# A two-layer encoder trunk on one core: another order of the seven products of a pair, and four powers on GpSimd at the start

## The chip, the core and the metric

The kernel runs on one core of one Trainium2 chip. The metric is the device time of one execution in microseconds. Five engines of the core matter here, each with an instruction queue of its own: TensorE (in profiles PE, with its weight loads as PEld), VectorE (DVE), ScalarE (ACT), GpSimd (POOL) and SyncE (SP), which here only issues DMAs. They wait for each other through semaphores. SBUF is the working memory, PSUM the memory into which TensorE writes, in banks.

## The reference

A trunk of two layers over 512 tokens of width 1024, in float32, with a memory of 256 tokens. Cut to what matters:

```python
for layer in range(2):
    xn = rms_norm(x, mix_norm[layer])
    x = x + (fox_diff_mixer if layer == 0 else mlstm_mixer)(xn, ...)
    x = x + memory_cross_attention(rms_norm(x, ...), rms_norm(mem, ...), ...)
    x = x + conv_ffn(rms_norm(x, ffn_norm[layer]), w_up, conv_w, conv_b, w_down)
return rms_norm(x, final_norm)

def conv_ffn(xn, w_up, conv_w, conv_b, w_down):
    h = causal_depthwise_conv(xn @ w_up, conv_w) + conv_b   # three taps along the tokens
    g, u = jnp.split(h, 2, axis=-1)                         # 2816 columns each
    return (jax.nn.gelu(g) * u) @ w_down
```

The change touches `conv_ffn`, in both layers, and the start of the program. `rms_norm` multiplies by the mean square to the power -0.5.

## The kernel before

**Numbers.** To keep float32 accuracy each operand is split into a high part, rounded to the float32r type, and a low part, the rest. ScalarE makes the high part by a copy (`split`, L282, or the casts at L1183 and L1352), VectorE the low part by a subtraction (`sub`, L279). A product of two operands is three matmuls (`mm3`, L289 to L291): high by high, high by low, low by high. Nearly every subtraction on VectorE has both of its inputs in SBUF.

**Start.** `constants()` makes the identity (on GpSimd), a tile of ones and a few others, and twelve small products on ones for TensorE to start with. Then the first mixer loads x, forms xh and xl (L491 on ScalarE, L492 on VectorE), the weights of the gates (L541 to L546) and the first value product, until the norm's factor is known. The powers of -0.5 of the norms are worked out on VectorE (`rsqrt`, L425 to L432): a first guess from the bits and three Newton steps, on a few columns. GpSimd makes causal masks in the mixers (L900, L1574), a few memsets, and in the feed-forward stage issues the DMAs that add one block of weights onto another (L1336).

**Feed-forward.** The 2 x 2816 columns of `w_up` are 22 pairs of blocks of 128, one block of g and one of u. A pair is computed in one of two ways. `plain` does two ordinary blocks of 8 x 3 matmuls over 512 tokens. `seven`, for the 16 pairs listed in SEVEN, sees the pair as a 2 x 2 block product (block g or u by half of the inner dimension, times half of the inner dimension by half of the tokens) and does it with seven products in place of eight, after Strassen and Winograd. A product is 4 x 3 matmuls over 256 tokens (`product`). The sums of weights that this needs are made beforehand by GpSimd's accumulating DMAs and by VectorE (sb, L1358 and L1364), the sums of x once per layer in `forms` (tiles t).

The seven products of a pair run through three PSUM banks and small sums between them. p1 opens bank X; ScalarE copies it, negated, to v (L1393). p6 opens bank Y; u2 = Y + v. p2 adds onto X, which gives c11 (ScalarE, L1406). p7 adds onto Y, after u2 has been read from it; u3 = Y + v. p5 opens bank R; c22 = u3 - R. p3 adds onto R, after c22 has read it; c12 = R - u2. p4 adds onto Y, after u3 has read it; c21 = Y + v. The sums u2, u3, c22, c12 and c21 are VectorE's (all at L1398). c11 to c22 fill a tile hs, which is scaled by the norm's factor (L1419); then `tail` does the taps, the gelu, the product with u and the split into ah and al (L1274 to L1298).

The second product, with `w_down`, goes in chunks of four pairs: for each chunk eight blocks (`down`, 4 x 3 matmuls over 512 tokens, added onto x at L512). They wait in a queue, filled at pairs 5, 9, 13 and 18; each call of `fill()` takes one. A `plain` pair calls it twice. A `seven` calls it three times: after p7's sums, after p4, and at the end of the pair.

**What sets the order.** `Sched` is a list planner. Every step is added with an engine, a planned duration, its dependencies, a priority (its due time) and the buffers that it takes and frees. For TensorE's steps the due time is `clock[0]`, which each step advances by its planned duration; other engines' steps and the loads are due at fixed distances from it. The planner simulates the engines with these durations and emits the steps; the framework below it puts in the semaphores and orders an engine's instructions by the order in which they were emitted and by when it takes them to be ready. The lines that carry the planned durations and the order are these:

```python
def pe(dur, fn, deps, take=(), free=()):
    clock[0] += dur
    return add("PE", dur, fn, deps, clock[0] - dur, take, free, 0.2)
last = pe(0.7 * per, fn, [lo, last, *deps], ...)   # a block, per = 4 or 2 inner steps
n = 1.42                                           # a product of a seven
```

The tile sq, of which there is one buffer, holds the running sum of squares for a norm. Its first use is at the norm of the memory, some way into the first mixer (L482).

Of the kernel before, what the change touches and what calls it, by code (L numbers as in the profile page):

```python
# [237 lines left out]
class Builder:  # L238
# [276 lines left out]
    def constants(self):  # L515
        nc, cp = self.nc, self.cp
        self.ident = cp.tile([P, P], F32, name="ident")
        make_identity(nc, self.ident[:])
        self.onesr = cp.tile([P, P], F32R, name="ones")
        self.ones = self.onesr[:].bitcast(F32)  # L520
        nc.vector.memset(self.ones[:], 1.0)
        self.ones2 = cp.tile([P, 2], F32, name="ones2")
        nc.vector.memset(self.ones2[:], 1.0)
        self.selc = cp.tile([P, 12], F32, name="selc")
        nc.vector.tensor_tensor(out=self.selc[:, 0:8], in0=self.ident[:, 0:8], in1=self.ident[:, 32:40], op=ALU.add)
        nc.vector.tensor_tensor(out=self.selc[:, 8:12], in0=self.ident[:, 64:68], in1=self.ident[:, 96:100], op=ALU.add)
        self.warm = cp.tile([P, 3], F32, name="warm")
        nc.scalar.activation(self.warm[:, :2], self.ones2[:], AF.Exp)
        ps = self.acc_bank(0)
        for _ in range(WARM):  # L530
            nc.tensor.matmul(ps[:, :P], self.ones[:], self.ones[:], start=True, stop=True)
        self.vec = cp.tile([P, NVEC], F32, name="vec")
        nc.scalar.dma_start(self.vec[:, :8], self.t["vec"][:, :8])
# [602 lines left out]
    def ffn_steps(self, layer, mp):  # L1136
# [15 lines left out]
# [3 lines that stand above are left out]
# [34 lines left out]
        def block(src, nk, xs, at, bank, deps, steps, tag="raw"):  # L1189

            st, lo = weight(src, nk * P, at, tag)
            last = None
            per = nk // steps
            for c in range(steps):

                def fn(c=c):
                    if c == 0:
                        st["ps"] = self.acc_bank(st["_acc"]) if bank == "acc" else self.bank(bank)
                    for k in range(c * per, (c + 1) * per):
                        s = slice(k * P, (k + 1) * P)  # L1200
                        xh, xl = xs(k)
                        self.mm3(st["ps"][:], st["wh"][:, s], st["wl"][:, s], xh, xl, k == 0, k == nk - 1)

                last = pe(0.7 * per, fn, [lo, last, *deps], [(bank, st)] if c == 0 else (), [("h", st)] if c == steps - 1 else ())
            return st, last

        own = lambda k: (self.xh[k][:], self.xl[k][:])
# [119 lines left out]
        def seven(p, fill):  # L1327
# [54 lines left out]
                st[bank] = self.acc_bank(b["_acc"]) if tag == "acc" else self.bank(tag)  # L1382
                product(*a)

            n = 1.42
            p1 = pe(n, lambda: opened("X", bx, "acc", f3, 0, *X(0, 0), "X", True), [w3], [("acc", bx)])
            p6 = pe(n, lambda: opened("Y", by, "acc", s2, 0, *T2, "Y", True), [w2, *formed], [("acc", by)], [("s2", s2)])
            p5 = pe(n, lambda: opened("R", br, "s", f1, 512, *T1, "R", True), [w1], [("s", br)])
            get = rows(st, at + 2.0)

            def v_():
# [8 lines left out]
            bank = lambda n_: (lambda: restored(st[n_][:, :256]))  # L1400
            tmp = lambda n_: (lambda: folded(st[n_][:]))
            hs = lambda j, l: (lambda: folded(st["hs_"][:, j, 2 + 256 * l : 258 + 256 * l]))
            v = add("ACT", act(256), v_, [p1], at + 1.5, [("v", bv)])
            u2 = add("DVE", 0.34, lambda: sum_("u2", tmp("u2"), bank("Y"), tmp("v_"), ALU.add), [p6, v], at + 4.0, [("u2", bu2)])
            p2 = pe(n, lambda: product(f3, 512, *X(1, 0), "X", False), [p1, v], (), [("h", f3)])
            c11 = add("ACT", act(256), lambda: nc.scalar.copy(hs(0, 0)(), bank("X")()), [p2, get], clock[0] + 2.0, (), [("acc", bx)])  # L1406
            p7 = pe(n, lambda: product(f1, 0, *T3, "Y", False), [u2, p5], (), [("h", f1)])
            u3 = add("DVE", 0.34, lambda: sum_("u3", tmp("u3"), bank("Y"), tmp("v_"), ALU.add), [p7], clock[0], [("u3", bu3)])
            c22 = add("DVE", 0.34, lambda: sum_(None, hs(1, 1), tmp("u3"), bank("R"), ALU.subtract), [u3, p5, get], clock[0], (), [("u3", bu3)])
            fill()  # L1410
            p3 = pe(n, lambda: product(s4, 0, *X(1, 1), "R", False), [c22, w4], (), [("s4", s4)])
            c12 = add("DVE", 0.34, lambda: sum_(None, hs(0, 1), bank("R"), tmp("u2"), ALU.subtract), [p3, get], clock[0], (), [("s", br), ("u2", bu2)])
            p4 = pe(n, lambda: product(a22, 0, *T4, "Y", False), [u3, w22], (), [("a22", a22)])
            c21 = add("DVE", 0.34, lambda: sum_(None, hs(1, 0), bank("Y"), tmp("v_"), ALU.add), [p4, get], clock[0], (), [("acc", by), ("v", bv)])
            fill()

            def scaled():
                h = st["hs_"][:, :, 2:514]
                tt_(out=h, in0=h, in1=self.rb[:].unsqueeze(1).to_broadcast([P, 2, 512]), op=ALU.mult)  # L1419

            m = add("DVE", 1.14, scaled, [c11, c22, c21, c12, normed], clock[0] + 2.0)
            fill()
            tail(p, st, [[m], [m]], clock[0] + 3.0)


# [408 lines left out]
```

## Time and profile before

| | us |
|---|---|
| median of 3 runs | 1455.07 |
| lowest and highest run | 1453.4, 1455.21 |
| the profiled execution | 1455.27 |
| its span, from the first to the last instruction | 1453.5 |
| TensorE busy | 1427.1 (98%) |
| VectorE busy | 1193.3 (82%) |
| ScalarE busy | 801.7 (55%) |
| GpSimd busy | 57.9 (4%) |

The granted TensorE clock was 0.998 over the span. All times in profile rows are counted from the span's start. A row of a timeline has the start, the duration, the engine, the line of the kernel, the operation, the tile written and the tiles read, the shape and a count; in brackets stands the engine's idle time before it and what ended that. A row of waits has who waited, for what, the total, the number of times and the longest. A row of windows has the stretch, its length, and for each engine its busy time and number of instructions. Matmuls are pipelined and their ends are modelled, so their lengths in a row overlap: the distance between two starts is what counts.

### The profile page before, as it was taken

The numbers are of one execution on the slowest core, as the hardware profiler recorded it, in microseconds if no ns is written. First come the engines' busy times: TensorE is split into PE (matmuls) and PEld (weight loads), VectorE is DVE, ScalarE is ACT, GpSimd is POOL, SyncE is SP. The second block draws the span as 40 slices with busy tenths as digits, with TensorE's granted clock in tenths as the row PEclk, the third lists the DMA queues.
The fourth block names the chain that finished last, engine by engine and source line by source line (L and its number), as shares of the span: only waits on it lengthen the run. The fifth ranks groups of instructions, "written<-read, shape, count | busy, mean of one in ns | idle before, by whom it ended". The sixth has DMA issues, their size and how long they took to land.

```text
span 1453.5 us, 22202 instructions
## 1 busy us (share of the span) xinstructions
PE 1427.1 (98%) x8330; PEld 1267.4 (87%) x8330; DVE 1193.3 (82%) x2255; ACT 801.7 (55%) x1345; POOL 57.9 (4%) x100
## 2 busy tenths in 40 slices
PE   9999999999999999999999999999999999999998
PEld 7888868899889999899888788889988899999987
DVE  7778886766689999999778868676667999999975
ACT  7767574444466555545456734444445655555544
POOL 0000120000001000000000100000000000000000
PEclk9999999999999999999999999999999999999999
DMA  5222304324248666542332232323323756564322
GB/s 200 88 73 73 102 32 158 117 86 131 87 138 196 172 156 166 145 131 66 94 103 87 74 102 78 111 91 127 117 87 123 200 156 168 159 160 133 89 70 80
DMA packets 60796, 171.74 MB, mean 118 GB/s; under 512 B 6673, under 2 KB 6673, under 8 KB 60689
## 3 DMA queue, kind: packets, MB, share of 16 engines
q1 hardware_dynamic: 55072, 152.43, 32.3%
q0 software_dynamic: 4608, 16.78, 6.9%
q8 instruction: 65, 1.06, 0.3%
q10 hardware_dynamic: 1008, 1.12, 0.2%
q14 instruction: 43, 0.34, 0.1%
HBM read 168.21 MB, written 2.10 MB: 117 GB/s over the span
## 4 chain that ended last, share of the span: by engine, by line
PE 68%; DVE 22%; issue 4%; ACT 4%; DMA 1%; POOL 0%; DVEq 0%; ACTq 0%; POOLq 0%
PE acc L289 13%; PE acc L291 13%; PE acc L290 13%; DVE wl L279 5%; DVE c L1281 4%; PE w L289 3%; PE w L290 3%; PE w L291 3%; PE acc L351 2%; PE s L289 2%; PE acc L352 2%; PE acc L353 2%; PE s L291 2%; PE s L290 2%; PE w L1621 1%
## 5 line engine op out<-in xcount | busy, mean ns | idle before, releaser
L289 PE MATMUL acc<-xh,wh 128*128 128x512 f32 (+1 forms) x832 | 293.3, 353 | 0.1
L291 PE MATMUL acc<-xh,wl 128*128 128x512 f32 (+1 forms) x832 | 289.1, 347 | 1.3 <-DVE wl L279 1.3
L290 PE MATMUL acc<-xl,wh 128*128 128x512 f32 (+1 forms) x832 | 289.0, 347 | 0.0
L279 DVE TENSOR_TENSOR wl<-raw,wh 128x1024 fp32r<-128x1024 f32 (+2 forms) x201 | 240.6, 1197 | 39.3 <-ACT wh L282 35.8
L282 ACT CAST wh<-raw 128x1024 fp32r<-128x1024 f32 (+2 forms) x137 | 140.3, 1026 | 156.2 <-PE acc L290 96.7
L291 PEld LDWEIGHTS acc<-xh,wl 128*128 128x128 f32 x832 | 158.2, 190 | 16.8 <-DVE wl L279 1.6
L289 PEld LDWEIGHTS acc<-xh,wh 128*128 128x128 f32 x832 | 158.2, 190 | 15.4 <-ACT v L1393 0.3
L290 PEld LDWEIGHTS acc<-xl,wh 128*128 128x128 f32 x832 | 158.2, 190 | 15.0
L1281 DVE SCALAR_TENSOR_TENSOR c<-hs,vec,c 128x512 f32<-128x512 f32 x176 | 129.3, 750 | 5.1 <-ACT c L1274 4.6
L289 PE MATMUL w<-ah,wh 128*128 128x512 f32 x304 | 115.6, 380 | 0.0
L291 PE MATMUL w<-ah,wl 128*128 128x512 f32 x304 | 115.3, 379 | 0.0
L290 PE MATMUL w<-al,wh 128*128 128x512 f32 x304 | 115.3, 379 | 0.0
L1274 ACT ACTIVATE c<-hs,vec 128x512 f32<-128x512 f32 x88 | 69.7, 812 | 56.5 <-DVE hs L1419 49.2
L291 PEld LDWEIGHTS w<-ah,wl 128*128 128x128 f32 x304 | 57.5, 189 | 8.1
L289 PEld LDWEIGHTS w<-ah,wh 128*128 128x128 f32 x304 | 57.7, 190 | 7.2 <-ACT c L1289 0.5
L290 PEld LDWEIGHTS w<-al,wh 128*128 128x128 f32 x304 | 57.7, 190 | 6.7
L289 PE MATMUL acc<-mem,wh 128*128 128x256 f32 (+1 forms) x192 | 60.3, 314 | 0.0
L291 PE MATMUL acc<-mem,wl 128*128 128x256 f32 (+1 forms) x192 | 59.8, 311 | 0.0
L290 PE MATMUL acc<-mem,wh 128*128 128x256 f32 (+1 forms) x192 | 59.6, 311 | 0.0
L512 DVE TENSOR_TENSOR x<-w,x 128x512 f32<-128x512 f32 x72 | 49.5, 688 | 9.1 <-PE w L291 9.1
L1183 ACT CAST wh<-dr 128x512 fp32r<-128x512 f32 x64 | 39.4, 615 | 31.1 <-PE w L290 15.3
L512 DVE TENSOR_TENSOR x<-acc,x 128x512 f32<-128x512 f32 x32 | 22.1, 691 | 40.4 <-PE acc L291 40.4
(373 smaller groups left out, 3758.5 us busy)
## 6 DMA issues: line engine op xcount, KB each, us to landing
raw<-in_up_dram SPq DMA_DIRECT2D x56, 512.0 KB, 3.3
dr<-in_down_dram SPq DMA_DIRECT2D x64, 256.0 KB, 2.9
sa<-in_up_dram SPq DMA_DIRECT2D x32, 512.0 KB, 4.2
sa<-in_up_dram POOLq DMA_DIRECT2D x32, 512.0 KB, 5.5
raw<-in_xk_dram SPq DMA_DIRECT2D x16, 512.0 KB, 3.3
raw<-in_wo_dram SPq DMA_DIRECT2D x16, 512.0 KB, 3.2
raw<-in_xq_dram SPq DMA_DIRECT2D x16, 512.0 KB, 3.3
raw<-in_xv_dram SPq DMA_DIRECT2D x16, 512.0 KB, 3.2
```

Source lines behind the costliest of these rows:

```text
L279: self.nc.vector.tensor_tensor(out=lo, in0=v, in1=hi.bitcast(F32), op=ALU.subtract)
L282: self.nc.scalar.copy(hi, v)
L289: mm(out, wh, xh, start=first, stop=False, skip_group_check=parts)
L290: mm(out, wh, xl, start=False, stop=False, skip_group_check=parts)
L291: mm(out, wl, xh, start=False, stop=last, skip_group_check=parts)
L351: mm(ps, xh[k][:, ts], wh, start=(k == 0), stop=False)
L352: mm(ps, xh[k][:, ts], wl, start=False, stop=False)
L353: mm(ps, xl[k][:, ts], wh, start=False, stop=(k == 7))
L512: self.nc.vector.tensor_tensor(out=x, in0=restored(ps[:]), in1=x, op=ALU.add)
L1183: nc.scalar.copy(st["wh"][:, :cols], st[tag][:, :cols])
L1274: nc.scalar.activation(st["c_"][:, j, :], hs()[:, j, 2:514], AF.Identity, scale=self.col("cw", (layer * 3 + 2) * 44 + blk), bias=self.col( ...
L1281: nc.vector.scalar_tensor_tensor(out=c, in0=hs()[:, j, n : n + 512], scalar=w, in1=c, op0=ALU.mult, op1=ALU.add)
```

## The change

At the start, in `constants()`, GpSimd fills the tile sq with -0.5 and raises ones to that power four times: for 4, 4 and 128 columns into a part of the tile, and for all 512 columns in place. Nothing reads the results; the tile is taken again for the sums of squares later.

In `seven` the products run in the order p1, p6, p2, p7, p5, p4, p3 (before: p1, p6, p5, p2, p7, p3, p4). Two calls of `fill()` stand inside, one ahead of p7 and one ahead of p4; the one at the end of the pair is gone. The small sums are added right behind the product that they read, with due times that follow from the clock at that point. The planned durations are 1.345 in place of 1.42 for a product, 0.65 in place of 0.7 for an inner step of a block, and 0.33 in place of 0.34 for a small sum. p5 and p7 share the weights f1; p7 now waits for these and u2 and no longer for p5, and p5, now the later one, frees them.

```diff
@@ -524,6 +524,13 @@
         self.selc = cp.tile([P, 12], F32, name="selc")
         nc.vector.tensor_tensor(out=self.selc[:, 0:8], in0=self.ident[:, 0:8], in1=self.ident[:, 32:40], op=ALU.add)
         nc.vector.tensor_tensor(out=self.selc[:, 8:12], in0=self.ident[:, 64:68], in1=self.ident[:, 96:100], op=ALU.add)
+        half = self.til(self.sp, "sq", bufs=1)
+        nc.gpsimd.memset(half[:], -0.5)
+        for n in (4, 4, 128):
+            nc.gpsimd.tensor_tensor(out=half[:, 384 : 384 + n], in0=self.ones[:, :n], in1=half[:, :n], op=ALU.pow)
+        nc.gpsimd.tensor_tensor(
+            out=half[:].rearrange("p (a b) -> p a b", b=P), in0=self.ones.unsqueeze(1).to_broadcast([P, 4, P]), in1=half[:].rearrange("p (a b) -> p a b", b=P), op=ALU.pow
+        )
         self.warm = cp.tile([P, 3], F32, name="warm")
         nc.scalar.activation(self.warm[:, :2], self.ones2[:], AF.Exp)
         ps = self.acc_bank(0)
@@ -1201,7 +1208,7 @@
                         xh, xl = xs(k)
                         self.mm3(st["ps"][:], st["wh"][:, s], st["wl"][:, s], xh, xl, k == 0, k == nk - 1)
 
-                last = pe(0.7 * per, fn, [lo, last, *deps], [(bank, st)] if c == 0 else (), [("h", st)] if c == steps - 1 else ())
+                last = pe(0.65 * per, fn, [lo, last, *deps], [(bank, st)] if c == 0 else (), [("h", st)] if c == steps - 1 else ())
             return st, last
 
         own = lambda k: (self.xh[k][:], self.xl[k][:])
@@ -1382,10 +1389,7 @@
                 st[bank] = self.acc_bank(b["_acc"]) if tag == "acc" else self.bank(tag)
                 product(*a)
 
-            n = 1.42
-            p1 = pe(n, lambda: opened("X", bx, "acc", f3, 0, *X(0, 0), "X", True), [w3], [("acc", bx)])
-            p6 = pe(n, lambda: opened("Y", by, "acc", s2, 0, *T2, "Y", True), [w2, *formed], [("acc", by)], [("s2", s2)])
-            p5 = pe(n, lambda: opened("R", br, "s", f1, 512, *T1, "R", True), [w1], [("s", br)])
+            n = 1.345
             get = rows(st, at + 2.0)
 
             def v_():
@@ -1400,26 +1404,28 @@
             bank = lambda n_: (lambda: restored(st[n_][:, :256]))
             tmp = lambda n_: (lambda: folded(st[n_][:]))
             hs = lambda j, l: (lambda: folded(st["hs_"][:, j, 2 + 256 * l : 258 + 256 * l]))
-            v = add("ACT", act(256), v_, [p1], at + 1.5, [("v", bv)])
-            u2 = add("DVE", 0.34, lambda: sum_("u2", tmp("u2"), bank("Y"), tmp("v_"), ALU.add), [p6, v], at + 4.0, [("u2", bu2)])
+            p1 = pe(n, lambda: opened("X", bx, "acc", f3, 0, *X(0, 0), "X", True), [w3], [("acc", bx)])
+            v = add("ACT", act(256), v_, [p1], clock[0], [("v", bv)])
+            p6 = pe(n, lambda: opened("Y", by, "acc", s2, 0, *T2, "Y", True), [w2, *formed], [("acc", by)], [("s2", s2)])
+            u2 = add("DVE", 0.33, lambda: sum_("u2", tmp("u2"), bank("Y"), tmp("v_"), ALU.add), [p6, v], clock[0], [("u2", bu2)])
             p2 = pe(n, lambda: product(f3, 512, *X(1, 0), "X", False), [p1, v], (), [("h", f3)])
             c11 = add("ACT", act(256), lambda: nc.scalar.copy(hs(0, 0)(), bank("X")()), [p2, get], clock[0] + 2.0, (), [("acc", bx)])
-            p7 = pe(n, lambda: product(f1, 0, *T3, "Y", False), [u2, p5], (), [("h", f1)])
-            u3 = add("DVE", 0.34, lambda: sum_("u3", tmp("u3"), bank("Y"), tmp("v_"), ALU.add), [p7], clock[0], [("u3", bu3)])
-            c22 = add("DVE", 0.34, lambda: sum_(None, hs(1, 1), tmp("u3"), bank("R"), ALU.subtract), [u3, p5, get], clock[0], (), [("u3", bu3)])
             fill()
+            p7 = pe(n, lambda: product(f1, 0, *T3, "Y", False), [u2, w1])
+            u3 = add("DVE", 0.33, lambda: sum_("u3", tmp("u3"), bank("Y"), tmp("v_"), ALU.add), [p7], clock[0], [("u3", bu3)])
+            p5 = pe(n, lambda: opened("R", br, "s", f1, 512, *T1, "R", True), [w1], [("s", br)], [("h", f1)])
+            c22 = add("DVE", 0.33, lambda: sum_(None, hs(1, 1), tmp("u3"), bank("R"), ALU.subtract), [u3, p5, get], clock[0], (), [("u3", bu3)])
+            fill()
+            p4 = pe(n, lambda: product(a22, 0, *T4, "Y", False), [u3, w22], (), [("a22", a22)])
+            c21 = add("DVE", 0.33, lambda: sum_(None, hs(1, 0), bank("Y"), tmp("v_"), ALU.add), [p4, get], clock[0] + 1.0, (), [("acc", by), ("v", bv)])
             p3 = pe(n, lambda: product(s4, 0, *X(1, 1), "R", False), [c22, w4], (), [("s4", s4)])
-            c12 = add("DVE", 0.34, lambda: sum_(None, hs(0, 1), bank("R"), tmp("u2"), ALU.subtract), [p3, get], clock[0], (), [("s", br), ("u2", bu2)])
-            p4 = pe(n, lambda: product(a22, 0, *T4, "Y", False), [u3, w22], (), [("a22", a22)])
-            c21 = add("DVE", 0.34, lambda: sum_(None, hs(1, 0), bank("Y"), tmp("v_"), ALU.add), [p4, get], clock[0], (), [("acc", by), ("v", bv)])
-            fill()
+            c12 = add("DVE", 0.33, lambda: sum_(None, hs(0, 1), bank("R"), tmp("u2"), ALU.subtract), [p3, get], clock[0], (), [("s", br), ("u2", bu2)])
 
             def scaled():
                 h = st["hs_"][:, :, 2:514]
                 tt_(out=h, in0=h, in1=self.rb[:].unsqueeze(1).to_broadcast([P, 2, 512]), op=ALU.mult)
 
             m = add("DVE", 1.14, scaled, [c11, c22, c21, c12, normed], clock[0] + 2.0)
-            fill()
             tail(p, st, [[m], [m]], clock[0] + 3.0)
 
 
```

## The prediction

> **What bounds the kernel now.** I read the page's first part, then the stages by windows, then who waited for whom on TensorE, and last the timeline of the first microseconds.
>
> ```profile
> span 1453.5 us, 22202 instructions
> PE 1427.1 (98%) x8330; PEld 1267.4 (87%) x8330; DVE 1193.3 (82%) x2255; ACT 801.7 (55%) x1345; POOL 57.9 (4%) x100
> ```
>
> The profiled execution took 1455.27 us: the span plus 1.8 us around it. The median of the runs shown is 1455.07 us, so a sum made against the profile also holds for the median to 0.2 us. TensorE (PE) is busy for 98% of the span. No edit here removes a matmul, so time can only come out of TensorE's waits, or be lost to new ones. The two places that the change touches, in windows: the head, where nothing runs on GpSimd (POOL) today, and the stretches of the two feed-forward stages that hold the pairs of seven products.
>
> ```profile
> core 0: us, PE busy (x) PEld busy (x) DVE busy (x) ACT busy (x) POOL busy (x), PEclk, DMA share, GB/s
> 5.00:25.00 20.00, 18.14 (x87) 13.81 (x86) 18.96 (x50) 15.64 (x26) 0.00 (x0) 1.00 0.74 262
> 430.00:695.00 265.00, 259.59 (x1838) 243.48 (x1836) 255.78 (x397) 146.23 (x225) 13.82 (x16) 1.00 0.56 148
> 1130.00:1400.00 270.00, 265.48 (x1864) 248.70 (x1863) 260.88 (x405) 148.71 (x229) 13.70 (x16) 1.00 0.55 146
> ```
>
> The reader should see two things. In the feed-forward stretches TensorE is idle for 265 - 259.59 = 5.4 us and 270 - 265.48 = 4.5 us, some 10 us in all: a better order of products cannot win much more. And VectorE (DVE) is busy for 255.78 of 265 and 260.88 of 270, so it is nearly a second bound; a new order only helps if VectorE's small sums come out at the right time. In the head VectorE is busy for 18.96 of 20 us: it has 1.04 us to spare.
>
> **Part 1, the products in another order.** What TensorE's weight loads waited for, over the whole program:
>
> ```profile
> engine line waited for: us in total, times, longest us
> PEld s L289 <- DVE hs L1398: 11.0, 18, 1.4
> PEld acc L289 <- DVE u L1398: 3.2, 6, 0.8
> PEld acc L291 <- DVE wl L279: 1.6, 2, 0.8
> ```
>
> The first row is product p3, which adds onto bank R and therefore waits until c22 has read R; c22 in turn waits for u3, and u3 for p7. One such wait, at a pair with no down block inside it, beside the length of a product:
>
> ```profile
> 515.59 0.28 PE L289 MATMUL acc<-xh,wh 128*128 128x256 f32 x1
> ...
> 516.93 0.28 PE L289 MATMUL acc<-th,s2h 128*128 128x256 f32 x1
> ...
> 518.16 0.28 PE L291 MATMUL acc<-th,s2l 128*128 128x256 f32 x1
> ...
> 518.66 0.38 PE L289 MATMUL s<-xh,s4h 128*128 128x256 f32 x1 [0.23 <-DVE hs L1398]
> ```
>
> Twelve matmuls from 515.59 to 516.93 make a product 1.34 us long, which is what the new planner constant 1.345 says (the old one was 1.42). The step from 518.16 to 518.66 is p3's start held up.
>
> The new order is p1, p6, p2, down block, p7, p5, down block, p4, p3. Between p6 and p7 (which needs u2) now stand p2 and a block, where p5 and p2 stood. Between u3 and p4 stand p5 and a block; between c22 and p3 stand at least p4 and often the block. The wait of the first row should nearly go. Its bound is 11.0 us.
>
> What comes late next: u2, u3 and c22 in the pairs that get no block. By the code a seven took up to three blocks before, so a queue of eight was used up in three pairs and pairs 8 and 12 had none, beside 4, 17 and 20. With two per pair, eight blocks last exactly four pairs, and only pairs 4, 17 and 20 are bare. There p7, p4 and p3 each have a single product of 1.34 us to cover a sum. I price such a pair with the longest wait of the second row, 0.8 us: 3 pairs x 2 layers x 0.8 = 4.8 us. The gain is 11.0 - 4.8 = 6.2 us, and I take 6. Bounds: the three rows together, 15.8 us, if every wait goes; and a loss of about 6 if each of the three sums in each bare pair waits 0.8 us and p3 gains little (3 x 3 x 2 x 0.8 = 14.4, less half of the 15.8).
>
> Edits costed at nothing: the planner's constants (1.42 to 1.345, 0.7 to 0.65) change only due times, by 5 to 7% of the distance between two steps. Loads stay in hand:
>
> ```profile
> raw<-in_up_dram SPq DMA_DIRECT2D x56, 512.0 KB, 3.3
> dr<-in_down_dram SPq DMA_DIRECT2D x64, 256.0 KB, 2.9
> ```
>
> They land in 3.3 and 2.9 us and are planned 9 us or more ahead. Each down block carries one such DMA on SP's queue; the blocks are spread over four pairs instead of three, which evens out that queue and VectorE's share of each block. The DMAs that POOL issues for the sums of the weights keep their place by due time. Chunk by chunk the ten activation buffers come free one pair later: pairs 0 to 8 hold nine, so the tenth still covers it. If that cover is gone, ScalarE's cast for the next pair waits, about one block.
>
> **Part 2, the powers on GpSimd.** The change puts on POOL a memset of 512 columns and four powers of 4, 4, 128 and 512 columns, 648 in all. No power runs in the trace. What stands nearest, on POOL:
>
> ```profile
> 0.88 0.53 POOL L597 MEMSET rows<- 128x512 f32 x1
> 1.44 0.29 POOL masks.py:199 TENSOR_SCALAR_AFFINE_SELECT ident<-ident 128x128 f32<-128x128 f32 x1
> 142.75 0.75 POOL L900 TENSOR_SCALAR_AFFINE_SELECT tb<-ta 128x128 f32<-128x128 f32 x1 [141.02 <-ACT ta L889]
> ...
> 172.73 1.43 POOL L900 TENSOR_SCALAR_AFFINE_SELECT tb<-ta 128x384 f32<-128x384 f32 x1 [6.78 <-DVE sm L676]
> ...
> 198.51 0.51 POOL L900 TENSOR_SCALAR_AFFINE_SELECT tb<-ta 128x384 f32<-128x384 f32 x1 [0.20 <-DVE sm L676]
> ...
> 208.75 0.30 POOL L900 TENSOR_SCALAR_AFFINE_SELECT tb<-ta 128x128 f32<-128x128 f32 x1 [1.96 <-ACT ta L889]
> ...
> 218.28 0.61 POOL L900 TENSOR_SCALAR_AFFINE_SELECT tb<-ta 128x512 f32<-128x512 f32 x1 [2.54 <-DVE sm L676]
> ```
>
> POOL's queue is empty from 1.73 to 142 us, so for POOL itself the powers are free. The question is VectorE. A 384-column select takes 0.51 us at 198.51 and 1.43 us at 172.73. VectorE at that time, and at another place where it came second:
>
> ```profile
> 172.58 1.22 DVE L279 TENSOR_TENSOR wl<-raw,wh 128x1024 fp32r<-128x1024 f32 x1
> ...
> 212.38 1.54 DVE L279 TENSOR_TENSOR wl<-raw,wh 128x1024 fp32r<-128x1024 f32 x1
> ```
>
> At 172.73 the select started behind VectorE's subtraction with two inputs in SBUF and was stretched by 0.9 us, until that had ended (172.58 + 1.22 = 173.80). At 212.38 it is the other way round: the same subtraction, 1.22 us alone, took 1.54 us, because a select was under way. So an instruction that reads SBUF on POOL and a two-input one on VectorE exclude each other, and the later one waits. The Trainium skill says this in "SBUF — State Buffer", section "Who interferes with whom": the port pair is an exclusive lock, held for the whole instruction, and the loser fully blocks. These rows agree with it for operations of about 1 us; none shows an operation of many microseconds, and if the port were only taken while data moves, a slow power would cost VectorE next to nothing.
>
> What VectorE does in the head, with the first use on TensorE:
>
> ```profile
> 4.59 0.75 DVE L492 SCALAR_TENSOR_TENSOR xl<-x,vec,xh 128x512 fp32r<-128x512 f32 x1 [0.25 <-ACT xh L491]
> 5.26 0.18 DVE L544 CAST wh<-gw 128x64 fp32r<-128x64 f32 x1
> ...
> 6.23 0.22 DVE L279 TENSOR_TENSOR wh<-gw,wh 128x64 fp32r<-128x64 f32 x1
> 6.61 0.38 PE L559 MATMUL w<-xh,wh 128*40 128x512 f32 x1
> ```
>
> TensorE's gate product at 6.61 follows the gate weights' subtraction at 6.23 with almost no slack, and all of VectorE's queue stands behind whichever instruction is blocked.
>
> How long is a power? Lower bound: one pass like the select, whose slope is (0.61 - 0.30) / 384 = 0.81 ns per column over 0.19 us fixed: 648 x 0.81 ns + 4 x 0.19 = 1.3 us, over by 3 us, cost nothing. For the other end I have the kernel's own power of -0.5, twelve elementwise instructions on VectorE:
>
> ```profile
> 168.23 0.16 DVE L426 TENSOR_SCALAR z<-s 128x2 f32<-128x2 f32 x1
> ...
> 170.19 0.16 DVE L432 SCALAR_TENSOR_TENSOR y<-a,y 128x2 f32<-128x2 f32 x1
> ```
>
> That is the special case of one exponent. A general power is a logarithm, a multiplication and an exponential with their special cases; I estimate 30 such passes, and bound it by 12 and 100. At 30 passes: 30 x 0.81 = 24 ns a column, 3.1 us for 128 columns, 12.4 us for 512, 0.2 for the two small ones, 0.8 fixed: 16.5 us. I take the value near the lower of the two ends because the twelve-instruction row is the nearest thing in the trace.
>
> Placed: POOL is at 1.73 us after the select of the identity, 2.3 with one memset more; the 128-column power ends at about 6.1. VectorE's first two-input instruction (4.59) gets in there, until 6.8; the 512-column power holds the port from 6.8 to 19.4. VectorE's next instruction, at 5.26 today, starts at 19.4: 14.1 us late, of which the idle 1.04 us are won back. TensorE follows VectorE directly, and behind the head it is full, so 13 us land on the end. Bounds: nothing (1.3 us of powers) and, at 100 passes (81 ns a column, 53 us), about 50 us.
>
> **Sum.** 1455.27 + 13 - 6 = 1462.3 for a profiled execution, 1462 for the median.
>
> **The rivals.**
> Faster: the powers are cheap, or VectorE gets the port between their reads. For it: POOL's rows are fast (0.61 us for 512 columns); against it: a power is no single pass, and the stretched 1.54 us row. Then only part 1 counts: 1455 - 6 = 1449. It decides from a total power time of 10 us downwards: with the end at 2.3 + 10 = 12.3, VectorE is 12.3 - 5.26 - 1.04 = 6 us late, as much as part 1 wins. By the rate that the Trainium skill states for an addition in "GPSIMD Engine Reference", section 3.1 (4497 ns for 2048 columns), the powers would take about 1.4 us by estimate and be over before VectorE needs the port; no run here shows a power at that rate.
>
> Much slower: a power worked lane by lane or unpipelined, above 45 us in all. The sum then follows its length: 1455 + 60 - 6 = 1509 at 63 us. It goes beyond the head if it lasts to 94.8 us, when ScalarE writes the same scratch tile:
>
> ```profile
> L482 ACT ACTIVATE sq<-raw x2: 399/400/401, 94.8 to 792.2; 128x256 f32<-128x256 f32 x2
> ```
>
> The order does not pay: VectorE is so full that u2 is late for p7 in the bare pairs. The price is the 6 us lost above, with the powers as forecast 1455 + 13 + 6 = 1474.
>
> **How the numbers follow.** I give the forecast 0.45 (1456 to 1490 by itself, for powers of 10 to 45 us), the cheap power 0.27 (1441 to 1452), the long power 0.16, the order that does not pay 0.12. A measurement of this kernel tells about 0.2%, 2.9 us. Of the forecast 0.08 lies within that, so slower has 0.37 + 0.16 + 0.12 = 0.65, same 0.08, faster 0.27. The range reaches down to 1445, leaving out about 0.07 of the cheap case, and up to 1505, leaving out about 0.11 of the long one.
>
> **What would show it.** Part 2: a POOL row of more than 10 us for the 512-column power near the start, beside it a VectorE two-input instruction of the same length, and a TensorE idle of that length ahead of the gate product, now at 6.61 us. Part 1: the row of p3's waits (11.0 us) down to a few, the row for u at most doubled, and shorter stretches between the first and last pair of seven. The prediction is wrong if the power row is under 8 us, or if VectorE's rows beside it keep their length of 0.75 us.

## The result, and the profile after

The changed kernel takes 1460.15 us, the median of 6 runs (1458.48 to 1461.48); the kernel before, on the same chip, takes 1453.57 us (6 runs, 1452.52 to 1455.21). The ratio is 1.0043 with a 95% interval of 1.0030 to 1.0056: slower by 6.2 us (4.4 to 8.1). The prediction was 1462 us, slower. The sum came out right, but the larger of its two terms came out for another reason than the one on record, by luck, and the trace shows that at once.

The profiled execution of after took 1458.48 us and was its fastest run; that of before, 1455.27 us, lies at the top of its runs. So the two profiles differ by 3.2 us only, where the medians differ by 6.6.

The page of after, first part and the chain of work that ended last by engine:

```profile
span 1456.7 us, 22220 instructions
PE 1424.8 (98%) x8330; PEld 1268.2 (87%) x8330; DVE 1190.0 (82%) x2255; ACT 798.5 (55%) x1345; POOL 163.6 (11%) x105
PE 70%; DVE 16%; POOL 7%; issue 3%; ACT 2%; DMA 1%; DVEq 0%; POOLq 0%; ACTq 0%
```

GpSimd (POOL) is busy for 163.6 us where it was 57.9, and it now holds 7% of the chain, about 100 us. What it does there, in the timeline of after, with the instructions behind it. (From L527 to the products of a pair, line numbers are 7 higher than in before; the small sums of L1398 stand at L1402, the copy v of L1393 at L1397. The row of two at 3.20 merges the second power over 4 columns with the one over 128, which the row at 4.28 shows alone.)

```profile
1.71 1.03 POOL L530 TENSOR_TENSOR sq<-ones,sq 128x4 f32<-128x4 f32 x1
...
3.20 21.87 POOL L530 TENSOR_TENSOR sq<-ones,sq 128x4 f32<-128x4 f32 x2
...
4.28 20.79 POOL L530 TENSOR_TENSOR sq<-ones,sq 128x128 f32<-128x128 f32 x1
...
25.15 82.48 POOL L531 TENSOR_TENSOR sq<-ones,sq 128x512 f32<-128x512 f32 x1
107.66 0.42 ACT L482 ACTIVATE sq<-raw 128x256 f32<-128x256 f32 x1 [12.48 <-POOL sq L531]
...
108.51 1.68 DVE L492 SCALAR_TENSOR_TENSOR mem<-raw,vec,mem 128x256 fp32r<-128x256 f32 x4 [12.06 <-ACT mem L491]
...
110.11 0.28 DVE L710 COPY pt<-w 128x128 f32<-128x128 f32 x1
...
110.45 0.69 PE L707 MATMUL w<-ident,x 128*128 128x128 f32 x2 [9.31 <-DVE pt L710]
...
111.36 0.63 PE L352 MATMUL acc<-wl,xh 128*128 128x512 f32 x1
...
111.78 0.63 PE L353 MATMUL acc<-wh,xl 128*128 128x512 f32 x1
...
115.49 0.38 PE L353 MATMUL acc<-wh,xl 128*128 128x512 f32 x1
```

The same write of sq in before:

```profile
94.76 0.40 ACT L482 ACTIVATE sq<-raw 128x256 f32<-128x256 f32 x1
```

The power over 512 columns lasts 82.48 us and ends at 107.63. ScalarE's first use of the scratch tile sq, at 94.76 before, waits for it until 107.66, 12.9 us later. ScalarE's queue stands behind that instruction: the casts of the memory that follow are late, VectorE is idle for 12.06 us, and TensorE for 9.31 us ahead of the transposes at 110.45. Then TensorE's matmuls of 512 columns are 0.43 us apart (111.36 to 111.78) in place of 0.21, until 115.2. The windows of this place, in before and in after:

```profile
95.00:112.00 17.00, 16.59 (x85) 13.65 (x83) 12.56 (x43) 6.19 (x12) 0.00 (x0) 1.00 0.19 63
112.00:117.00 5.00, 4.66 (x23) 3.66 (x23) 3.74 (x11) 3.52 (x8) 0.00 (x0) 1.00 0.30 105
```

```profile
5.00:25.00 20.00, 18.73 (x89) 14.47 (x88) 18.72 (x50) 15.28 (x25) 20.00 (x1) 1.00 0.73 265
95.00:112.00 17.00, 7.69 (x37) 6.25 (x36) 4.48 (x15) 4.49 (x10) 12.63 (x1) 0.80 0.10 32
112.00:117.00 5.00, 5.00 (x19) 4.08 (x18) 3.25 (x10) 0.01 (x1) 0.00 (x0) 0.67 0.33 105
439.65:704.65 265.00, 261.37 (x1853) 245.94 (x1852) 257.14 (x402) 146.60 (x228) 13.88 (x16) 1.00 0.55 148
1136.10:1406.10 270.00, 266.34 (x1877) 250.43 (x1876) 261.45 (x409) 149.98 (x233) 13.71 (x16) 1.00 0.54 146
```

The 0.67 of the stretch from 112 to 117 us is an average. Cut where the granted clock changes, the same place in after reads:

```profile
101.69:105.10 3.41, 0.00 (x0) 0.00 (x0) 0.00 (x0) 0.00 (x0) 3.41 (x1) 1.00 0.00 0
105.10:111.93 6.83, 1.48 (x5) 1.30 (x6) 2.96 (x13) 4.24 (x9) 2.53 (x1) 0.50 0.00 0
111.93:115.34 3.41, 3.41 (x10) 2.69 (x9) 3.20 (x10) 0.08 (x1) 0.00 (x0) 0.50 0.39 114
115.34:118.75 3.41, 3.41 (x23) 3.10 (x22) 0.85 (x4) 0.00 (x0) 0.00 (x0) 1.00 0.10 40
```

The clock is 0.50 from 105.10 to 115.34 us. TensorE works at it from 110.45 on, so the wait costs some 2 us on top of itself. In the head (5 to 25 us), where the prediction had put the loss, VectorE's busy time is 18.72 us against 18.96 and TensorE's 18.73 against 18.14: nothing is lost. The feed-forward stretches are set later by 9.65 and 6.1 us, as these stages begin later; in the same length they hold 15 and 13 matmuls more than before, and TensorE's idle time in them falls from 5.4 and 4.5 us to 3.6 and 3.7.

TensorE's waits by weight loads, in after:

```profile
PEld w L707 <- DVE pt L710: 9.4, 1, 9.4
PEld acc L289 <- DVE u L1402: 6.1, 8, 1.9
...
PEld acc L289 <- ACT v L1397: 2.6, 2, 1.4
```

p3's waits for c22 (11.0 us before) are out of the list's first rows. The waits for u have gone from 3.2 to 6.1 us, and waits for v are new in these rows.

### The profile page after: what moved, and what is told of

Same layout as the page of the kernel before. It is cut to its first block, busy times and chain, and to the rows that moved or that the text cites. A ratio compares the mean times of both kernels' runs of the same rounds, so it can differ in the third digit from the quotient of the medians.

```text
span 1456.7 us, 22220 instructions
## 1 busy us (share of the span) xinstructions
PE 1424.8 (98%) x8330; PEld 1268.2 (87%) x8330; DVE 1190.0 (82%) x2255; ACT 798.5 (55%) x1345; POOL 163.6 (11%) x105
## 4 chain that ended last, share of the span: by engine, by line
PE 70%; DVE 16%; POOL 7%; issue 3%; ACT 2%; DMA 1%; DVEq 0%; POOLq 0%; ACTq 0%
PE acc L289 14%; PE acc L291 14%; PE acc L290 14%; POOL sq L531 6%; PE w L289 4%; PE w L291 4%; PE w L290 4%; DVE wl L279 3%; DVE c L1288 3%; PE s L289 2%; PE s L291 2%; PE s L290 2%; PE acc L351 2%; PE acc L352 2%; PE acc L353 2%
## 5 line engine op out<-in xcount | busy, mean ns | idle before, releaser
L290 PE MATMUL w<-al,wh 128*128 128x512 f32 x304 | 115.2, 379 | 0.0
L291 PE MATMUL w<-ah,wl 128*128 128x512 f32 x304 | 115.2, 379 | 0.0
L1343 POOL DMA_DIRECT2D sa<-in_up_dram x32 | 27.6, 862 | 514.2 <-DVE tl L279 128.2
L531 POOL TENSOR_TENSOR sq<-ones,sq 128x512 f32<-128x512 f32 x1 | 82.5, 82482 | 0.1
L1302 ACT CAST ah<-c 128x512 fp32r<-128x512 f32 x44 | 27.3, 620 | 65.4 <-DVE c L1298 65.4
```

What stands on the lines that cost most here:

```text
L290: mm(out, wh, xl, start=False, stop=False, skip_group_check=parts)
L291: mm(out, wl, xh, start=False, stop=last, skip_group_check=parts)
L531: nc.gpsimd.tensor_tensor(out=half[:].rearrange("p (a b) -> p a b", b=P), in0=self.ones.unsqueeze(1).to_broadcast([P, 4, P]), in1=half[:]. ...
L1343: return add("POOL", 0.0029 * cols, lambda: nc.gpsimd.dma_start(out(), src(), accum_op=ALU.add), deps, due, (), (), 6.0)
```

## Where the time went, place by place

The same matmul (by its number among the 8330) starts in each kernel so many microseconds later (or, with a minus, earlier) than in the profile of before. The columns are places in the time of before; 405 to 700 and 1105 to 1400 are the two feed-forward stages. The rows below after are the experiments that follow.

| profile of | 20 | 115 | 198 | 215 | 405 | 700 | 1105 | 1400 | end |
|---|---|---|---|---|---|---|---|---|---|
| after | 0.4 | 11.5 | 11.5 | 9.7 | 9.7 | 6.2 | 6.1 | 3.3 | 3.2 |
| e1: order only | 0.5 | 0.5 | 0.5 | -1.2 | -1.2 | -4.1 | -3.8 | -6.7 | -6.8 |
| e2: powers only | 0.5 | 11.0 | 11.0 | 10.8 | 10.8 | 9.6 | 9.6 | 10.1 | 10.4 |
| e3: own tile | 0.1 | 0.1 | 0.1 | -1.7 | -1.7 | -5.3 | -5.4 | -7.5 | -7.6 |
| e4: 384 columns | 0.3 | 0.3 | 0.2 | -1.6 | -1.6 | -5.2 | -5.3 | -7.1 | -7.3 |
| e5: power twice | -0.1 | 93.5 | 93.5 | 91.7 | 91.7 | 89.1 | 89.0 | 86.5 | 86.4 |
| e6: old durations | 0.0 | 0.0 | 0.0 | -1.6 | -1.6 | -4.9 | -4.6 | -7.3 | -7.3 |
| e7: new durations alone | 0.5 | 0.5 | 0.5 | 0.3 | 0.3 | 0.0 | -0.1 | 0.1 | 0.0 |
| e8: three blocks | 0.1 | 0.1 | 0.1 | 0.1 | 0.1 | -2.2 | -2.3 | -3.8 | -3.9 |
| e9: old order, two blocks | 0.4 | 0.3 | 0.3 | -1.3 | -1.3 | -2.2 | -2.3 | -2.6 | -2.7 |
| e10: p5 early in bare pairs | 0.8 | 0.7 | 0.7 | 0.7 | 0.7 | -2.9 | -2.6 | -5.2 | -5.4 |
| e11: before again | 0.2 | 0.2 | 0.2 | -1.4 | -1.4 | -1.9 | -1.9 | -0.3 | -0.3 |

In after, the loss of 11 us arises at one place, between 95 and 115 us, and the two feed-forward stages win 3.4 and 2.8 us. The step between 198 and 215 us is neither of the two; it is explained by e11.

Theory T, from this trace: the powers cost what ScalarE waits for the tile sq, and nothing else; the order wins about what was predicted. Rival P, the one on record: the powers hold the memory port that GpSimd shares with VectorE, so the cost goes with their length, in whatever tile.

## Experiments on the powers

**e1, the order without the powers.** Edit of after:

```diff
-        half = self.til(self.sp, "sq", bufs=1)
-        nc.gpsimd.memset(half[:], -0.5)
-        for n in (4, 4, 128):
-            nc.gpsimd.tensor_tensor(out=half[:, 384 : 384 + n], in0=self.ones[:, :n], in1=half[:, :n], op=ALU.pow)
-        nc.gpsimd.tensor_tensor(
...
```

> The changed kernel without the powers: new order, new planned durations and two down blocks per pair alone. Tile theory (the powers cost only because ScalarE must wait for scratch tile sq): TensorE loses what it lost at 110 us in the changed kernel, 11 to 12 us, less the half microsecond that it can win back, so 1447 to 1449 us against 1453.6 before; TensorE's wait of 9.4 us at 110 us is gone, and ScalarE writes sq at 95 us again. Port theory (the powers hold the memory port and VectorE stands): the same time, because it also takes all of the loss out; this run tells what the order is worth, predicted 6 us, and no more. If the order is worth nothing: 1453.

1448.67 us (9 runs, 1447.52 to 1451.42) against 1452.43 for before: ratio 0.9972 (0.9962 to 0.9981), 4.1 us faster (2.8 to 5.5). ScalarE writes sq at 95.2 us, and TensorE's wait at 110 us is gone. The order is worth 4 us. For the powers the medians give 1460.15 - 1448.67 = 11.5 us, but they come from two sessions, in which before differs by 1.1 us; each against its own before, it is 6.2 + 4.1 = 10.3 us. Call it 11. This kernel beats both. Its windows answer to the ones in the prediction, its waits to those of before:

```profile
430.00:695.00 265.00, 260.95 (x1850) 245.50 (x1849) 256.59 (x402) 145.89 (x227) 13.82 (x16) 1.00 0.55 148
1130.00:1400.00 270.00, 266.45 (x1877) 250.49 (x1876) 261.55 (x410) 149.99 (x233) 13.71 (x16) 1.00 0.54 144
```

```profile
PEld acc L289 <- DVE u L1395: 7.1, 14, 1.9
...
PEld acc L289 <- ACT v L1390: 3.1, 3, 1.2
```

TensorE is idle for 4.05 and 3.55 us there, where it was 5.4 and 4.5. The largest waits that are left are for the sums u2 and u3 (tile u) and for v.

**e2, the powers without the order.** The powers of after, put into before.

```diff
+        half = self.til(self.sp, "sq", bufs=1)
+        nc.gpsimd.memset(half[:], -0.5)
+        for n in (4, 4, 128):
...
```

> The kernel before with the powers in front, in scratch tile sq, and the old order of products. Both theories: before plus 11.5 us, about 1465 us, because the old order has no more slack in the feed-forward stage than the new one. If parts of the loss at 110 us are won back behind it (the changed kernel is 9.7 us late at the first feed-forward stage), 1460 to 1463.

1465.54 us (4 runs): ratio 1.0087 (1.0074 to 1.0101), slower by 12.6 us (10.7 to 14.7). The loss is 11 us at 115 us and still 10.4 us at the end (row e2 of the table), so the two parts of the change add up.

**e3, the powers in a tile of their own.** The same memset and four powers, on a tile that nothing else uses, at the start of the first mixer:

```diff
-        half = self.til(self.sp, "sq", bufs=1)
...
+            half = mp.tile([P, 512], F32, name="half")
...
```

> The changed kernel with the powers in a tile of their own, which nothing else writes or reads; the same memset and the same four powers. Tile theory: POOL's row of 82 us stays, ScalarE writes sq at 95 us again, TensorE's wait of 9.4 us at 110 us goes, and the time is that of the kernel without the powers to 0.5 us (1447 to 1449). Port theory (or any other disturbance by a busy GpSimd): the loss stays in full, 1460.

1448.66 us (9 runs, 1447.35 to 1452.64), ratio 0.9976 (0.9966 to 0.9985): the time of the kernel without any power. In its timeline the power is as long as in after, and sq is written at its old time:

```profile
25.14 82.25 POOL L752 TENSOR_TENSOR half<-ones,half 128x512 f32<-128x512 f32 x1
...
94.88 0.40 ACT L482 ACTIVATE sq<-raw 128x256 f32<-128x256 f32 x1
```

P falls: GpSimd is at it for 105 us, and the program loses nothing. VectorE's instructions with two inputs in SBUF beside the powers, grouped by line and shape from 5 to 95 us (busy time, then mean ns of one, then idle), in e3 and then in e1, which has no powers:

```profile
L279 DVE TENSOR_TENSOR wl<-raw,wh 128x1024 fp32r<-128x1024 f32 x15 | 18.3, 1219 | 3.2 <-ACT wh L282 3.2
L492 DVE SCALAR_TENSOR_TENSOR xl<-x,vec,xh 128x512 fp32r<-128x512 f32 x8 | 6.0, 746 | 0.3 <-ACT xh L491 0.3
...
L571 DVE TENSOR_TENSOR sqt<-sqt,rb 8x512 f32<-8x512 f32 x1 | 1.0, 979 | 0.1
```

```profile
L279 DVE TENSOR_TENSOR wl<-raw,wh 128x1024 fp32r<-128x1024 f32 x15 | 18.3, 1219 | 3.2 <-ACT wh L282 3.2
L492 DVE SCALAR_TENSOR_TENSOR xl<-x,vec,xh 128x512 fp32r<-128x512 f32 x8 | 6.0, 747 | 0.7 <-ACT xh L491 0.7
...
L571 DVE TENSOR_TENSOR sqt<-sqt,rb 8x512 f32<-8x512 f32 x1 | 0.7, 680 | 0.1
```

Fifteen subtractions of 1219 ns are 1219 ns beside the power as well. One single instruction is longer, by 0.3 us, and it runs about 1 us behind the start of the long power.

**e4, 384 columns in place of 512 in the last power.** Still in sq.

```diff
-            out=half[:].rearrange("p (a b) -> p a b", b=P), in0=self.ones.unsqueeze(1).to_broadcast([P, 4, P]), in1=half[:].rearrange("p (a b) -> p a b", b=P), op=ALU.pow
+            out=half[:, :384].rearrange("p (a b) -> p a b", b=P), in0=self.ones.unsqueeze(1).to_broadcast([P, 3, P]), in1=half[:, :384].rearrange("p (a b) -> p a b", b=P), op=ALU.pow
```

> The changed kernel with the last power over 384 columns in place of 512. By the row of 20.8 us for 128 columns it lasts 62 us and ends at 25 + 62 = 87 us, 8 us ahead of ScalarE's first write of sq at 94.8. Tile theory: nothing of the loss is left, 1447 to 1449, as with the tile of its own. Port theory (the loss goes with the length of the power): a quarter less than 11.5 us, 1457.

1448.28 us (6 runs, 1447.83 to 1448.95), ratio 0.9968 (0.9957 to 0.9980): nothing is lost, with the same tile.

```profile
25.14 61.99 POOL L531 TENSOR_TENSOR sq<-ones,sq 128x384 f32<-128x384 f32 x1
...
95.00 0.40 ACT L482 ACTIVATE sq<-raw 128x256 f32<-128x256 f32 x1
```

The power ends at 87.1 us, 8 us ahead of the tile's next use. A quarter less of the power took away the whole loss, not a quarter of it.

**e5, the last power twice.** Also in sq.

```diff
+        nc.gpsimd.tensor_tensor(
+            out=half[:].rearrange("p (a b) -> p a b", b=P), in0=self.ones.unsqueeze(1).to_broadcast([P, 4, P]), in1=half[:].rearrange("p (a b) -> p a b", b=P), op=ALU.pow
+        )
```

> The changed kernel with the power over 512 columns issued twice, so that the powers end at about 107.6 + 82.5 = 190 us in place of 107.6. Tile theory: behind 94.8 us each microsecond of power is a microsecond lost, 1460 + 82 = 1542 us, with one wait of some 90 us on TensorE. Port theory: the loss per power doubles from 11.5, 1472 us. A second thing can come in: GpSimd is then busy past 142 us, where its masks are due; they are behind the same wait, so nothing more than a few us.

1541.51 us (2 runs): 81.4 us above after, for 82.14 us more of power.

```profile
107.37 82.14 POOL L534 TENSOR_TENSOR sq<-ones,sq 128x512 f32<-128x512 f32 x1
...
189.54 0.42 ACT L482 ACTIVATE sq<-raw 128x256 f32<-128x256 f32 x1 [94.70 <-POOL sq L534]
```

Past the time at which ScalarE wants the tile, each microsecond of power costs a microsecond; up to there it costs nothing (e4). With e3 this settles the half of T that is on the powers.

## Experiments on the order

**e6 and e7, the planned durations.** e6 is e1 with the old ones (also 0.7 and 0.34), e7 is before with the new ones. The diff is that of e6; e7 has it the other way round.

```diff
-            n = 1.345
+            n = 1.42
```

> The new order without the powers, but with the planner's old durations (1.42, 0.7 and 0.34 for 1.345, 0.65 and 0.33). Order theory (the order of the products and the two blocks in between win the time, as predicted): the time of the new order without powers, to 1 us (1447 to 1449). Rival (the planner's durations win it, since the due times then fit TensorE's pace and no stage runs ahead of its plan): 1452 to 1454.

> The old order, with only the planner's new durations. Order theory: no change, 1453 to 1454.5. Rival (durations win it): 1447 to 1449.

e6: 1449.65 us (7 runs), ratio 0.9969 (0.9958 to 0.9980), as e1. e7: 1455.67 us (11 runs) against 1453.48, ratio 1.0011 (1.0002 to 1.0019), 1.6 us slower (0.3 to 2.8). The durations win nothing, alone or with the order, and alone may cost a little; that they are "at nothing" stands within that.

**e8 and e9, how many blocks stand in a pair.** e8 is e1 with a third `fill()` at the end of a seven; e9 is e7 (the old order) without its last one. The diff is that of e8; e9 takes the same line out.

```diff
+            fill()
             tail(p, st, [[m], [m]], clock[0] + 3.0)
```

> The new order without the powers, with a third place for a down block at the end of a pair, so that blocks are used up in three pairs again and pairs 8 and 12 have none either. My step that spread the blocks at nothing but said that bare pairs cost a wait at p7: the new order has 3 bare pairs in a layer, with three blocks it has 5; in the changed kernel the bare pairs cost 1.9 us (pair 17) and 1.7 us (pair 4), so 2 pairs x 2 layers x 1.8 = 7 us more than the new order alone: 1454 to 1456. If the place of the blocks does not matter: 1447 to 1449.

> The old order of the seven products with the new durations and two places for a down block in place of three, so that the blocks last four pairs and pairs 8 and 12 are no longer bare. Order theory (p3 behind p4 and the block between u3 and c22 win the time): p3 still waits for c22 in every pair, no gain, 1453 to 1456. Rival (the even spread of the blocks wins it): 1449 to 1451. The run with three blocks in the new order lost about 2 us of the gain of 4, so a part each is possible: 1451 to 1452.

e8: 1452.08 us (12 runs), ratio 0.9987 (0.9979 to 0.9995), 1.9 us faster than before, where the new order with two blocks is 4.1 to 4.5. So the third block takes away about half of the gain; I had expected all of it. e9: 1453.69 us (12 runs) against 1453.84, ratio 0.9998 (0.9988 to 1.0008): two blocks in the old order win nothing. What TensorE waits for, in e8 and in e9:

```profile
PEld acc L289 <- ACT v L1390: 9.5, 13, 1.2
```

```profile
PEld s L289 <- DVE hs L1398: 14.1, 22, 1.1
```

In e8 five pairs in a layer are bare, but the two that are newly so, 8 and 12, wait for nothing. By the starts of the matmuls the new waits, 0.6 us each for v at p2, stand in both layers in pairs 6, 10 and 14, each of which takes three blocks and follows a pair with three. So the new waits go with the third block in a pair and not, as I had expected, with the lack of blocks in others; why v is late there wasn't tested. In e9 p3 waits for c22 as ever, 22 times in place of 18. The new order takes p3's wait away, and with two blocks in a pair fewer others take its place. Either alone is worth 2 us or nothing.

**e10, p5 ahead of p2 in the bare pairs.** From e1:

```diff
+            bare = p < 5 or not queue
+            if bare:
+                p5 = pe(n, lambda: opened("R", br, "s", f1, 512, *T1, "R", True), [w1], [("s", br)])
             p2 = pe(n, lambda: product(f3, 512, *X(1, 0), "X", False), [p1, v], (), [("h", f3)])
...
+            if not bare:
+                p5 = pe(n, lambda: opened("R", br, "s", f1, 512, *T1, "R", True), [w1], [("s", br)], [("h", f1)])
```

> The new order without the powers, and in the pairs that get no block (4, 17, 20) product p5 ahead of p2, so that p7's wait for u2 is covered by two products. In the run without the powers TensorE loses some 1.5 us in pair 4 and 2.5 us in pair 17 of each layer. If the missing cover is what makes them (theory): pair 17's wait at p7 of 1.9 us falls by a product of 1.34 us to about 0.5, and p4, now with nothing between it and u3, waits 0.7 us in its place; pair 4 gains about 0.7. Together 0.7 + 0.7 in each layer, 2 to 3 us less than the new order alone: about 1446. Rival (the sums are late because VectorE is full, whatever the order): no gain, 1448 to 1449.

1449.89 us (5 runs) against 1453.84, ratio 0.9964 (0.9951 to 0.9977): not to be told from e1. By the starts of the matmuls p7's wait in pair 17 of the first layer fell from 1.89 to 1.09 us and p2's of 0.58 there went, but pair 20, which had waited for nothing, now waits 0.79 us at p4, and pair 4 stays at 1.2. No gain was made, as the rival had it; whether VectorE's full queue is the reason wasn't shown.

**e11, before once more.**

> The kernel before once more, for its profile. In the first profile the granted clock is 0.5 for about 2 us at 200 us, behind a lull of TensorE at 196 us, and TensorE loses 1.6 us there; the changed kernel and five of its variants do not show that, three other kernels do. If that is chance from one execution to the next, this profile can come without it, and its span is then 1451 to 1452 us. If it belongs to the kernel's own order, the clock falls again at 200 us and the span is 1453 to 1454 us.

1454.97 us, span 1453.2. The clock's fall at 200 us is absent this time. Windows of the first profile of before, then of the second:

```profile
198.00:200.00 2.00, 2.00 (x5) 0.59 (x5) 1.67 (x11) 1.87 (x8) 1.25 (x3) 0.68 0.03 8
200.00:202.00 2.00, 2.00 (x5) 0.80 (x6) 0.41 (x1) 0.13 (x2) 0.14 (x1) 0.50 0.00 0
```

```profile
198.00:200.00 2.00, 1.92 (x6) 0.88 (x7) 1.86 (x13) 1.86 (x7) 1.15 (x3) 1.00 0.00 0
200.00:202.00 2.00, 2.00 (x13) 1.17 (x13) 1.47 (x6) 1.04 (x4) 1.01 (x2) 1.00 0.00 0
```

The granted clock was 0.68 and 0.50 in the one and 1.00 in the other: 5 matmuls against 13 in the same 2 us. So it is chance from one execution to the next, and worth 1.6 us (the table's step from 198 to 215 us). The traces also show what the chance is in. Wherever the granted clock changes in a profile of this case, it changes a whole number of steps of 3.41 us after the change before. Here is the lull cut at these steps, in the first profile of before, then in the second:

```profile
195.30:198.71 3.41, 1.65 (x9) 1.01 (x9) 3.23 (x11) 3.35 (x6) 0.60 (x2) 1.00 0.02 5
198.71:202.12 3.41, 3.41 (x7) 0.96 (x9) 1.60 (x10) 1.29 (x6) 0.88 (x2) 0.50 0.00 0
```

```profile
193.48:196.89 3.41, 2.22 (x18) 1.82 (x17) 3.35 (x6) 3.33 (x8) 1.02 (x2) 1.00 0.02 5
196.89:200.30 3.41, 2.85 (x11) 1.39 (x11) 2.91 (x15) 3.25 (x9) 1.45 (x3) 1.00 0.00 0
```

In the first the lull lies within one step, with TensorE busy for 1.65 us of it, and the next step runs at 0.50; in the second it is spread over two, with 2.22 and 2.85 us. All thirteen profiles divide in this way: five with about 1.66 us in one step lose the 1.6 us, and in the other eight no step here has less than 1.99 us. The span, however, was not 1451 to 1452 as I had expected: the second feed-forward stage of this execution was 1.6 us longer than in the first. Over both stages the old order scatters from -1.2 to +1.1 us between the profiles of before, e2, e7, e9 and e11.

## Why the prediction was right or wrong, point by point

**The direction and the sum.** 1462 predicted, 1460.15 measured. The sum was +13 for the powers and -6 for the order; measured by e1 they are +10.3 to +11.5 and -4.1 (2.8 to 5.5). That 13 and 11 lie close together is luck: the 13 were worked out from a wait that did not come.

**Part 1, the order: right, somewhat too large.** The row of p3's waits went, and the row for u rose from 3.2 to 6.1 us, within the doubling. The first profile of before against that of e1 gives 2.9 us for each feed-forward stage, 5.8 in all, close to the 6; the medians give 4.1. A single pair of profiles can't decide between the two, since the old order scatters by some 1 us either way; the medians of many runs go before it. Of the term's parts, the bare pairs were priced at 0.8 us each, 4.8 us in all; by the starts of the matmuls in e1, pairs 4 and 17 lost 1.5 and 2.5 us in the first layer, 1.5 and 1.9 us in the second, and pair 20 nothing. But most of this isn't a cost of the new order: in before these pairs lose 1.2 and 1.6 us in the first layer and 1.2 and 1.8 in the second, so e1 loses some 1.6 us more there, not 4.8. Most of pair 4's loss is p2's wait for v, which the prediction didn't name, and it stands in e7 as well, which has the old order. What else kept the gain below the 11 us of p3's waits was not split up.

**"Edits costed at nothing".** The planner's durations are nothing (e6, e7). The spread of the blocks over four pairs is not: taken back, it costs half of the gain (e8). The prediction counted its effect only as the number of bare pairs and set the rest at nothing; in e8 the waits come up in pairs that take three blocks.

**Part 2, the powers: the loss right in size by luck, wrong in place and cause.** The failed step is "the 512-column power holds the port from 6.8 to 19.4. VectorE's next instruction, at 5.26 today, starts at 19.4". (By its own rule the cast at 5.26, with one input, would not have been held, only the two-input row at 6.23; that takes 1 us off the 13.) The prediction said that it would be wrong "if VectorE's rows beside it keep their length of 0.75 us", and they did. In after's timeline:

```profile
5.21 0.18 DVE L551 CAST wh<-gw 128x64 fp32r<-128x64 f32 x1
5.55 0.69 DVE L279 TENSOR_TENSOR wl<-raw,wh 128x512 fp32r<-128x512 f32 x1 [0.16 <-ACT wh L282]
...
6.72 0.76 DVE L492 SCALAR_TENSOR_TENSOR xl<-x,vec,xh 128x512 fp32r<-128x512 f32 x1 [0.34 <-ACT xh L491]
...
7.21 0.38 PE L566 MATMUL w<-xh,wh 128*40 128x512 f32 x1
```

All of these run while the power over 128 columns is at work (4.28 to 25.07), with their usual lengths. The gate product at 7.21 is 0.6 us later than before, and that is not the powers either: at 20 us e1, which has none, is 0.5 us late, and e5, which has the most, 0.1 us early.

The length was a second miss: 105 us in all against an estimate of 16.5 and an upper end of 53. It rested on 30 passes for a power, a number that no run shows; by the 161 ns per column measured, a power is some 200 times the 0.81 ns of a select's pass. Two errors met. With the measured length and the port held for all of it, the sum would have been about 1455 + 100 - 6 = 1549 us; with the estimated length and no lock, 1449. What decided was a sentence in a rival's margin: the loss "goes beyond the head if it lasts to 94.8 us, when ScalarE writes the same scratch tile". It did last that long, it was that tile, and it cost 12.9 us at ScalarE. I had the mechanism in hand and gave it no term, because my estimate of the length ended far ahead of it.

**The rivals.** Cheap powers (1449): the powers were dear, but the half of that rival by which VectorE gets the port in between was right, and e3 and e4 stand at its time, 1448.7 and 1448.3 us. Much slower (1509 at 63 us): in e4 the powers last until 87.1 us, over 80 us in all, and cost nothing. The order that doesn't pay (1474): no, by e1.

**The lock on the port.** The prediction quoted the Trainium skill, "SBUF — State Buffer", section "Who interferes with whom", for a lock held for the whole instruction, and noted that no row showed an operation of many microseconds. e3 now shows one: that VectorE is locked out for the whole of a power of 82 us the trace doesn't bear out, with subtractions of 1219 ns beside it and 1219 ns without. The select rows of about 1 us, from which the lock was argued, stay as they were.

## What to carry to other kernels

Ask of each new instruction not only which engine and port it takes, but which tile it writes and who writes that tile next: here a result that nobody reads cost about 11 us, because its scratch tile had another user, and a tile of its own made the same 105 us of work free. An operation for which the trace has no row should be timed by itself before it is placed; an upper end made from rows of other operations was too low by half. And when products wait on small sums, test the order of the products and the place of the work between them together: the order and the spread of the blocks were worth 4 us together, and 2 and nothing alone, and the waits came up in other pairs than the sum had them in.

## What the runs showed of the hardware

- A power on GpSimd costs 161 ns per column of 128 partitions: 20.79 us for 128 columns, 61.99 for 384, 82.48 for 512. A select over 512 columns takes 0.61 us there.
- Such a power leaves VectorE's two-input instructions at their usual length for all but about a microsecond: one instruction in 90 us was 0.3 us longer. When GpSimd reads its operands, and whether in pieces, wasn't tried.
- A wait of 9.3 us on TensorE was followed by matmuls at 0.43 us in place of 0.21, from 110.8 to 115.2 us, with a granted clock of 0.50 until 115.34 us.
- The granted clock changed only at whole numbers of steps of 3.41 us: it was 0.50 for one step in the first profile of before (198.71 to 202.13 us), for three in after (105.10 to 115.34 us) and for 27 in e5 (105.31 to 197.47 us). A much shorter lull, at 196 us, cost a step at 0.50 where it lay within one step, with TensorE busy for about 1.66 of its 3.41 us, and nothing where no step had less than 1.99 us, in the same kernel (before and e11) and over all thirteen profiles. How the clock's rule weighs work within a step wasn't tried, and the ends of matmuls are modelled. The Trainium skill, "TensorE: Matmul & The Clock Gate", section "Part 1: The HAM clock gate", states that the clock is set by the activity in a free-running window of about 3.4 us; these profiles agree with that.
